# Keys and values of the second memory attention made in the mix and held in DRAM

## The chip, the core and the metric

The kernel runs on one core of one Trainium2 chip. The time is device microseconds of one execution. Three runs of the kernel before took 2700.62, 2703.43 and 2705.85 us, a median of 2703.43 us. A further execution was profiled; all rows below are from it.

## What is computed

Two transformer blocks stand one behind the other, over 512 positions of 1024 features, all in float32. The first has two layers of attention. The second is the one the change is about:

```python
mem_n = rms_norm_2(mem, norm_mem)
h = rms_norm_2(x, norm_mix[l])
p_rw, p_s5, p_gla, p_gate = _split_2(h @ w_in[l], IN_SIZES)
y_rw, y_s5, y_gla = rwkv7_mix(p_rw, ...), s5_mix(p_s5, ...), gla_mix(p_gla, ...)
gates = jax.nn.sigmoid(p_gate).reshape(B, L, N_BRANCH, D_MODEL)
merged = sum(gates[:, :, i] * (y_i @ w_branch[l, i]))
x = x + merged @ w_out[l]
x = x + cross_attention(rms_norm_2(x, norm_xattn[l]), mem_n, xa_wq[l], xa_wkv[l], xa_wo[l])
x = x + conv_ffn(rms_norm_2(x, norm_ffn[l]), ...)
```

In `cross_attention` the queries come from `x`, so from everything before. The keys and values are `mem_n @ wkv`: 256 memory positions, 4 heads of 256 features. They need the kernel's inputs alone.

## The kernel before

Features lie on the 128 partitions, positions along the free axis, in tiles of 128 x 512. A product is made of three TensorE passes (`mm3`, lines 282 to 284): every operand is split into a high part, which ScalarE rounds, and a low part, which VectorE subtracts, and the passes are high by high, high by low, low by high. Weights are split too. `load_split` (lines 307 to 315) loads 256 KB into one of 7 raw buffers (`wraw`) through the queue of SyncE, ScalarE makes `wh` (line 312), VectorE makes `wl` (line 314), each in one of 5 buffers. One such load feeds 12 passes of 512 columns in most of the kernel. For keys and values it feeds 12 passes of 256 columns, because there are 256 memory positions.

The second block's stages are `mix`, `cross` and `ffn`. In `mix` the first branch (RWKV) is the main line of the code: `rwkv_a` for two pairs of heads, then the inverse of small triangles (`rwkv_invert`, 30 dependent steps on VectorE, lines 1506 and 1507), then `rwkv_b` four times. These steps wait on each other, so the code puts other products between them. They come from jobs: generators that yield the TensorE time of the products they have just issued. `push` puts a job in a list, with a kind (0, 1 or 2) and a stream, which names the pool of tiles that it allocates from. `fill(us)` takes products out of the jobs until about that much time has been issued; when no job is ready it gives up, and the main line's next step follows at once. A job that yields a negative number is not ready until the plan's clock has gone on so far. Kind 2 comes first, and kinds 0 and 1 take turns. So the order in which TensorE meets its work is set when the program is built. The framework that builds it then moves independent instructions of one engine past each other, and each engine runs its own list in order.

Jobs of kind 0 in the mix are: the low-rank inputs of RWKV, the gates and merge of branch 1, of branch 2, and the gates of branch 0. Jobs of kind 1 are the S5 branch and behind it the GLA branch. After the last `rwkv_b`, `flush` issues what is left of the jobs, then come the merge of branch 0 (`merge_g`, lines 2206 to 2226) and the product with `w_out`, which adds to `x` (line 1342). Between the four chunks of `w_out` the job `memory` loads and normalises the memory.

In `cross`, head 0's keys, values and queries are made first, in this order. For heads 1 to 3 the queries, keys and values are jobs, and `fill(4.5)` puts their products between the attention's steps; half of the output projection is a job as well. Tiles are allocated from pools by letter, and the last line of the setup of the mix is

```python
kit.room("abcc", a=22, b=11, c=54-22-11)
```

which gives the main line 22 tiles (`a`), jobs of kind 0 11 tiles (`b`), and kinds 1 and 2 together 21 (`c`). `cross` keeps these pools and sends all jobs to `c` (`SFLOW = "accc"`).

Of the kernel before, what the change touches and what calls it, by code (L numbers as in the profile page):

```python
# [10 lines left out]
F32 = mybir.dt.float32  # L11
F32R = mybir.dt.float32r
AF = mybir.ActivationFunctionType
ALU = mybir.AluOpType
# [3 lines left out]
S = 512  # L18
D = 1024
DT = D // 128  # L20
MEM = 256
# [14 lines left out]
BOTH = {"mm": "mm ch si", "si": "si", "ch": "ch"}  # L36
X_BOTH = {"mm": "mm ch", "si": "si", "ch": "mm ch"}
LATE = {"mm": "mm", "si": "si", "ch": "ch", "tr": "ch"}, dict(mm=3, ch=3, si=2)
SFLOW = "accc"
AB_FILL, CD_FILL, X_FILL = (0.9, 1.2), (1.15, 1.3, 1.1), (1.1, 1.4)  # L40


# [607 lines left out]
def tok(b):  # L650
    return lambda a: a[:, b * 128 : b * 128 + 128]
# [3 lines left out]
DENSE_K = [(j * 128, 128, [0, 1, 2, 3]) for j in range(4)]  # L655
# [664 lines left out]
class Second:  # L1320
# [908 lines left out]
    def mix(self):  # L2229
        kit, I = self.kit, self.I  # L2230
        self.xs = kit.xs
        self.merged, self.gates, self.O = {}, {}, []
        gla, s5 = [], []

        def branch1():
            yield from self.s5_g(s5, lambda: kit.push(branch2(), kind=1))
            kit.push(self.merge_g(1, s5, g1))
            self.g2 = kit.push(self.gates_g(2))

        def branch2():  # L2240
            yield from self.gla_g(gla)
            kit.push(self.merge_g(2, gla, self.g2))
            self.g0 = kit.push(self.gates_g(0))

        kit.push(branch1(), kind=1)
        lora = kit.push(self.rwkv_lora())
        g1 = kit.push(self.gates_g(1))
        kit.fill(20.0)
        kit.need(lora)
        rw = self.rwkv()  # L2250
        kit.flush()
        kit.run(self.merge_g(0, rw, self.g0))
        job = kit.push(self.memory(), kind=2, stream=1)
        for c in range(4):
            kit.fill(3, 10)
            kit.run(kit.proj_g(I["w_out"][c], self.O, lambda i, p: self.add(2 * c + i, p, "norm_xattn")))
        kit.need(job)


    def memory(self):  # L2260

        kit, nc, I = self.kit, self.nc, self.I
        ms = self.ms = []
        mems = [kit.load("", src=src) for src in I["mem2T"]]
        yield -6
        for m in range(DT):
            if m % 2 == 0:
                mem, hl = mems[m // 2], kit.u()
            c = slice(m % 2 * MEM, m % 2 * MEM + MEM)
            ms.append([z[:, c] for z in hl])  # L2270
            kit.split_scaled(mem[:, c], self.vec("norm_mem", m), *ms[m])
            if m == 0:
                acc = kit.f(MEM)
                nc.scalar.square(acc, mem[:, c])
            else:
                sq = kit.f(MEM)
                nc.scalar.square(sq, mem[:, c])
                nc.gpsimd.tensor_tensor(acc, acc, sq, op=ALU.add)
            yield -1
        self.mr = kit.t([128, 2], "mr2", 1)  # L2280
        nc.vector.tensor_copy(self.mr, kit.rpow(kit.sums(acc, kit.ones, [tok(0), tok(1)]), 1.0 / D, EPS))
        big = kit.spread_begin(self.mr, 2)
        yield -4
        self.mrb = kit.spread_end(big)

    def cross(self):
        kit, nc, I = self.kit, self.nc, self.I
        xs, ms, mr, mrb = kit.xs, self.ms, self.mr, self.mrb
        st, O = {}, {}
        sc = kit.small(4, "scq")  # L2290

        def keys(h):
            def emit(j, p):
                if not j:
                    hl = kit.u()
                    st["k", h] = [[z[:, j * MEM : j * MEM + MEM] for z in hl] for j in range(2)]
                f = kit.f(MEM)
                nc.vector.tensor_tensor(f, p, mrb, op=ALU.mult)
                kit.split(f, *st["k", h][j])

            yield from kit.proj_g(I["xa_wk"][h], ms, emit)

        def vals(h):
            st["v", h] = []

            def emit(b, p):
                st["v", h].append(kit.u(256))
                kit.split_scaled(p, mr[:, b : b + 1], *st["v", h][b])

            yield from kit.proj_tok_g(I["xa_wv"][h], ms, [tok(0), tok(1)], emit)  # L2310

        def query(h):
            st["q", h] = []

            def emit(j, p):
                st["q", h].append(kit.u())
                if not h and not j:
                    nc.vector.tensor_scalar(sc, kit.rstd(), 256.0**-0.5, None, op0=ALU.mult)
                kit.split(p, *st["q", h][j])

            yield from kit.proj_g(I["xa_wq"][h], xs, emit)

        def out(ts, g=None):
            for t in ts:
                if isinstance(O[t], list):
                    kit.need(O[t])
            for c in range(4):
                w = I["xa_wo"][c][:, :, ts[0] : ts[-1] + 1]
                yield from kit.proj_g(w, [O[t] for t in ts], lambda i, p: self.add(2 * c + i, p, g))

        def done(h, sums):
            s = []

            def end():
                big = kit.inverse(sums)
                yield -2
                rb = kit.spread_end(big)
                for j in range(2):
                    nc.vector.tensor_tensor(s[j], s[j], rb, op=ALU.mult)
                    hl = kit.u()  # L2340
                    kit.split(s[j], *hl)
                    O[2 * h + j] = hl

            def f(outs):
                for j in range(2):
                    s.append(kit.f())
                    nc.scalar.copy(s[j], outs[j])
                O[2 * h] = O[2 * h + 1] = kit.push(end(), True)
                if h == 1:
                    kit.push(out(range(0, 4)))  # L2350

            return f

        kit.run(keys(0))
        kit.run(vals(0))
        kit.run(query(0))
        jobs = [[]] + [[kit.push(g(h)) for g in (query, keys, vals)] for h in range(1, 4)]

        def heads():
            for h in range(4):  # L2360
                kit.need(*jobs[h])
                qk = []
                for (qh, ql), (kh, kl) in zip(st["q", h], st["k", h]):
                    qk += [(qh, kh), (qh, kl), (ql, kh)]
                sums = kit.small(4, "sums")
                soft = kit.soft_full(sc, [sums[:, b : b + 1] for b in range(4)])
                yield Head(kit, qk, st["v", h], [(0, 256)] * 4, DENSE_K[:2], soft, done(h, sums), 4.5)

        kit.attention(heads())
        kit.flush()  # L2370
        kit.run(out(range(4, 8), "norm_ffn"))
# [94 lines left out]
def program(tc, ctx, I, out):  # L2466
    kit = Kit(tc, ctx, I)
# [25 lines left out]
    f.ffn(1, take)  # L2493
    kit.need(job)
    done()
    kit.room("abcc", a=22, b=11, c=54-22-11)
    s.reset = kit.load("reset")
    s.mix()
    kit.flow(SFLOW)
    s.cross()  # L2500
    kit.room("aaaa", a=50)
    s.ffn()
# [14 lines left out]
```

## Time and profile before

| | |
|---|---|
| median of three runs | 2703.43 us (2700.62 to 2705.85) |
| the profiled execution | 2697.67 us |
| its span, first to last instruction | 2695.9 us |
| mean granted TensorE clock | 0.978 of full |
| TensorE busy / weight loads / VectorE / ScalarE / GpSimd | 95% / 77% / 59% / 44% / 19% |

The stages of the second block in the span: the mix's projections and `rwkv_a` until 1650 us, the inverse until 1721, `rwkv_b` until 2068, the merge and `w_out` until 2135, `cross` until 2284, and `ffn` behind it. A matmul's end in the profile is modelled and lies past the start of the next one, so two matmuls that follow each other without a pause look like 100% busy; the distance between their starts is what one costs.

### The profile page before, as it was taken

Reading aid. Unit: us, or ns where it says so; the run is one execution under the profiler, and the core shown is the slowest. Engines: PE = TensorE matmul, PEld = TensorE weight load, DVE = VectorE, ACT = ScalarE, POOL = GpSimd, SP = SyncE. Lnnn points to the kernel's source line nnn. Section 1 sums busy time; section 2 is a strip of 40 time slices with the busy share of each in tenths; the row PEclk is TensorE's granted clock in tenths of the full one; section 3 lists DMA queues with packets and bytes.
Section 4 is the critical chain, followed back from the end, with each engine's and each line's share of the span. In section 5 each row is a group of like instructions: output and inputs, shape, how many; then the busy total and the mean of one; then the engine's idle time right before and its main releaser. Section 6 shows DMA issues by size and latency. Waiting matters only on the chain. (4 is left out here: it accounts for less than half of the span.)

```text
span 2695.9 us, 37069 instructions
## 1 busy us (share of the span) xinstructions
PE 2573.7 (95%) x13432; PEld 2083.8 (77%) x13432; DVE 1594.7 (59%) x3076; ACT 1180.1 (44%) x2208; POOL 518.9 (19%) x439
## 2 busy tenths in 40 slices
PE   8999999999999999999999989799999999999998
PEld 6668778888776787787877767587777798888886
DVE  5686654344457876876335477654464656774673
ACT  5576543233445765332334322435233445543443
POOL 5325021010211131143103232112231300100001
PEclk9999999999999999999999989899999999999999
DMA  4112223333322131334433553421222333233332
GB/s 155 36 51 87 67 85 93 101 97 93 116 89 71 44 98 47 114 118 145 126 106 110 167 170 98 102 97 60 71 79 70 119 119 97 83 97 95 98 94 70
DMA packets 172520, 258.51 MB, mean 96 GB/s; under 512 B 42528, under 2 KB 60832, under 8 KB 172320
## 3 DMA queue, kind: packets, MB, share of 16 engines
q1 hardware_dynamic: 172336, 256.13, 31.2%
q8 instruction: 106, 1.74, 0.3%
q14 instruction: 78, 0.64, 0.1%
HBM read 234.04 MB, written 22.15 MB: 95 GB/s over the span
## 5 line engine op out<-in xcount | busy, mean ns | idle before, releaser
L312 ACT CAST wh<-wraw 128x512 fp32r<-128x512 f32 (+1 forms) x777 | 473.3, 613 | 886.4 <-PE ps_mm L283 606.9
L314 DVE TENSOR_TENSOR wl<-wraw,wh 128x512 fp32r<-128x512 f32 (+1 forms) x691 | 491.7, 715 | 355.5 <-ACT wh L312 343.5
L284 PE MATMUL ps_mm<-xs,wl 128*128 128x512 f32 x1544 | 612.6, 397 | 22.4 <-DVE wl L314 21.5
L282 PE MATMUL ps_mm<-xs,wh 128*128 128x512 f32 x1544 | 623.2, 404 | 9.0 <-ACT wh L312 8.3
L283 PE MATMUL ps_mm<-xs,wh 128*128 128x512 f32 x1544 | 612.6, 397 | 3.0 <-DVE xs L264 2.9
L284 PEld LDWEIGHTS ps_mm<-xs,wl 128*128 128x128 f32 x1544 | 293.8, 190 | 89.6 <-DVE wl L314 24.1
L282 PEld LDWEIGHTS ps_mm<-xs,wh 128*128 128x128 f32 x1544 | 294.1, 190 | 76.4 <-ACT wh L312 8.7
L283 PEld LDWEIGHTS ps_mm<-xs,wh 128*128 128x128 f32 x1544 | 293.6, 190 | 66.2 <-DVE xs L264 6.4
L448 POOL TENSOR_TENSOR acc<-acc,za 128x512 f32<-128x512 f32 x59 | 82.0, 1391 | 729.5 <-ACT za L444 728.2
L282 PE MATMUL ps_mm<-za,wh 128*128 128x512 f32 x460 | 183.2, 398 | 5.6 <-ACT za L248 5.6
L284 PE MATMUL ps_mm<-za,wl 128*128 128x512 f32 x460 | 182.3, 396 | 4.1 <-DVE wl L314 4.1
L283 PE MATMUL ps_mm<-za,wh 128*128 128x512 f32 x460 | 180.7, 393 | 0.2 <-DVE za L245 0.2
L314 POOL TENSOR_TENSOR wl<-wraw,wh 128x512 fp32r<-128x512 f32 x86 | 112.5, 1316 | 304.9 <-ACT wh L312 300.1
L1193 POOL TENSOR_TENSOR za<-za,za 128x512 f32<-128x512 f32 x44 | 60.0, 1364 | 462.0 <-ACT za L1192 462.0
L284 PEld LDWEIGHTS ps_mm<-za,wl 128*128 128x128 f32 x460 | 87.5, 190 | 24.5 <-DVE wl L314 4.5
L282 PEld LDWEIGHTS ps_mm<-za,wh 128*128 128x128 f32 x460 | 87.6, 190 | 24.3 <-ACT za L248 6.4
L282 PE MATMUL ps_mm<-zb,wh 128*128 128x512 f32 (+1 forms) x284 | 100.4, 354 | 4.4 <-ACT zb L248 4.4
L283 PEld LDWEIGHTS ps_mm<-za,wh 128*128 128x128 f32 x460 | 87.3, 190 | 20.5 <-DVE za L245 1.0
L245 DVE TENSOR_TENSOR za<-ps_tr,za 128x512 fp32r<-128x512 f32 (+3 forms) x152 | 84.6, 558 | 31.2 <-ACT za L248 29.9
L283 PE MATMUL ps_mm<-zb,wh 128*128 128x512 f32 (+1 forms) x284 | 97.4, 344 | 0.1
L284 PE MATMUL ps_mm<-zb,wl 128*128 128x512 f32 (+1 forms) x284 | 97.3, 343 | 0.0
L468 POOL TENSOR_TENSOR rs<-sm,neghalf 128x4 f32<-128x4 f32 (+2 forms) x32 | 45.3, 1416 | 240.3 <-DVE sm L467 240.3
(590 smaller groups left out, 4768.2 us busy)
## 6 DMA issues: line engine op xcount, KB each, us to landing
wraw<-w_gu SPq DMA_DIRECT2D x176, 256.0 KB, 2.7
wraw<-w_dn SPq DMA_DIRECT2D x96, 256.0 KB, 2.6
wraw<-w_up SPq DMA_DIRECT2D x88, 256.0 KB, 2.6
wraw<-w_gate SPq DMA_DIRECT2D x48, 256.0 KB, 2.8
wraw<-w_dn SPq DMA_DIRECT2D x48, 192.0 KB, 2.3
dram<-za SPq DMA_DIRECT2D x26, 256.0 KB, 2.5
zc<-dram SPq DMA_DIRECT2D x26, 256.0 KB, 4.5
wraw<-w_cd SPq DMA_DIRECT2D x24, 256.0 KB, 2.7
```

The lines of the kernel that those rows point to most:

```text
L245: self.nc.vector.tensor_tensor(lo, src, hi.bitcast(F32), op=ALU.subtract)
L282: mm(out, ah, bh, start=start, stop=False, **kw)
L283: mm(out, ah, bl, start=False, stop=False, **kw)
L284: mm(out, al, bh, start=False, stop=stop, **kw)
L312: self.nc.scalar.copy(hl[0], raw)
L314: eng.tensor_tensor(hl[1], raw, hl[0].bitcast(F32), op=ALU.subtract)
L448: self.nc.gpsimd.tensor_tensor(self.acc[0], self.acc[0], sq, op=ALU.add)
L468: self.nc.gpsimd.tensor_tensor(r, ms, self.neghalf[:, :n], op=ALU.pow)
L1193: nc.gpsimd.tensor_tensor(a, a, st["rb"], op=ALU.mult)
```

## The change

Keys and values of all four heads become one job of the mix, `memory_kv`, of kind 0, put in the list behind the low-rank job and ahead of the gates of branch 1. It first needs the job `memory`, which is now pushed at the start of the mix. Each finished tile pair (high and low) is stored to a DRAM scratch of 4 heads x 4 tiles of 256 KB, and the store is issued when the first half of the next tile is done (`late`, `store`). Behind the merge of branch 0 the 16 tiles are loaded back into the 18 tiles of pool `b`, for which `SFLOW` makes it stream 2. `cross` then makes queries alone. Its fill is 2.7 in place of 4.5.

```diff
-SFLOW = "accc"
+SFLOW = "acbc"
+C_FILL = 2.7
...
         lora = kit.push(self.rwkv_lora())
+        kit.push(self.memory_kv(kit.push(self.memory(), kind=2, stream=1)))
         g1 = kit.push(self.gates_g(1))
...
         kit.run(self.merge_g(0, rw, self.g0))
-        job = kit.push(self.memory(), kind=2, stream=1)
+        kit.flow(SFLOW)
+        self.kv = []
+        for h in range(4):
+            self.kv.append([kit.r(stream=2) for _ in range(4)])
+            for z, d in zip(self.kv[h], self.kv_dram[h]):
+                kit.nc.sync.dma_start(z.bitcast(F32), d)
         for c in range(4):
-            kit.fill(3, 10)
             kit.run(kit.proj_g(I["w_out"][c], self.O, lambda i, p: self.add(2 * c + i, p, "norm_xattn")))
-        kit.need(job)
...
     def memory(self):
-        mems = [kit.load("", src=src) for src in I["mem2T"]]
-        yield -6
         for m in range(DT):
             if m % 2 == 0:
-                mem, hl = mems[m // 2], kit.u()
+                mem, hl = kit.load("", src=I["mem2T"][m // 2]), kit.u()
+                yield -4
...
+    def memory_kv(self, job):
+        kit, nc, I = self.kit, self.nc, self.I
+        self.kv_dram = self.scratch([4, 4, 128, S])
+        kit.need(job)
+        late = []
+        def store():
+            for z, d in late:
+                nc.sync.dma_start(d, z.bitcast(F32))
+            late.clear()
+        def keys(h):
+            hl = []
+            def emit(j, p):
+                if not j:
+                    hl[:] = kit.u()
+                c = slice(j * MEM, j * MEM + MEM)
+                f = kit.f(MEM)
+                nc.vector.tensor_tensor(f, p, self.mrb, op=ALU.mult)
+                kit.split(f, *(z[:, c] for z in hl))
+                if j:
+                    late.extend((z, self.kv_dram[h, i]) for i, z in enumerate(hl))
+                else:
+                    store()
+            return kit.proj_g(I["xa_wk"][h], self.ms, emit)
+        def vals(h):
...
+        for h in range(4):
+            yield from keys(h)
+            yield from vals(h)
+        yield -3
+        store()
...
     def cross(self):
-        kit.run(keys(0))
-        kit.run(vals(0))
         kit.run(query(0))
-        jobs = [[]] + [[kit.push(g(h)) for g in (query, keys, vals)] for h in range(1, 4)]
+        jobs = [[]] + [[kit.push(query(h))] for h in range(1, 4)]
...
-                yield Head(kit, qk, st["v", h], [(0, 256)] * 4, DENSE_K[:2], soft, done(h, sums), 4.5)
+                yield Head(kit, qk, st["v", h], [(0, 256)] * 4, DENSE_K[:2], soft, done(h, sums), C_FILL)
...
-    kit.room("abcc", a=22, b=11, c=54-22-11)
+    kit.room("abcc", a=22, b=18, c=21)
     s.reset = kit.load("reset")
     s.mix()
-    kit.flow(SFLOW)
     s.cross()
```

Three places show how the order moves. Names are the program's (`wh`, `wl` weights, `xs` the normed input, `zb` and `zc` tiles of the pools, `ps_` PSUM banks); lines of the changed kernel below line 38 are one higher.

TensorE at the end of S5's second half, beside the inverse. Before, the next work is the first projection of GLA (`ps_mm_16169`):

```order
L2159 MATMUL ps_si_15939<-zc_15906,zc_16058 128x63
L2159 MATMUL ps_si_15940<-zc_15906,zc_16058 128x63
L282 MATMUL ps_mm_16169<-xs_13673,wh_16159 128x512
L283 MATMUL ps_mm_16169<-xs_13674,wh_16159 128x512
L284 MATMUL ps_mm_16169<-xs_13673,wl_16160 128x512
```

Now a tile of keys of the last head stands there (`zb_14203` and `zb_14204` are the memory's high and low part):

```order
L2160 MATMUL ps_si_16055<-zc_16035,zc_16258 128x63
L283 MATMUL ps_mm_16278<-zb_14203,wh_16268 128x256
L284 MATMUL ps_mm_16278<-zb_14204,wh_16268 128x256
L2160 MATMUL ps_si_16054<-zc_16032,zc_16303 128x63
L2160 MATMUL ps_si_16055<-zc_16032,zc_16303 128x63
L285 MATMUL ps_mm_16278<-zb_14203,wl_16269 128x256
L283 MATMUL ps_mm_16278<-zb_14203,wh_16268 128x256
```

Between the last `rwkv_a` and the first `rwkv_b`, 192 of the 384 products of keys and values now stand on TensorE; the gates of branch 1, which stood there, come later.

VectorE at the end of the inverse, before. The split of the weights that GLA's projection reads (`wl_16160`) stands behind the last step:

```order
L1506 TENSOR_TENSOR zc_15794<-zc_15793 128x58
L1511 MEMSET zc_15793 128x16
L1507 TENSOR_TENSOR zc_15793<-zc_15793,zc_15794 128x2x29
L1506 TENSOR_TENSOR zc_15794<-zc_15793 128x30
L1507 TENSOR_TENSOR zc_15793<-zc_15793,zc_15794 128x30
L314 TENSOR_TENSOR wl_16160<-wraw_16157,wh_16159 128x512
```

Now splits of weights and of keys stand between the steps (a stretch of the middle):

```order
L1507 TENSOR_TENSOR zc_16133<-zc_16132,zc_16131 128x192
L315 TENSOR_TENSOR wl_16269<-wraw_16266,wh_16268 128x512
L315 TENSOR_TENSOR wl_16275<-wraw_16272,wh_16274 128x512
L1508 TENSOR_TENSOR zc_16132<-zc_16132,zc_16133 128x16x12
L1507 TENSOR_TENSOR zc_16133<-zc_16131 128x26
L315 TENSOR_TENSOR wl_16336<-wraw_16333,wh_16335 128x128
L1508 TENSOR_TENSOR zc_16131<-zc_16131,zc_16133 128x2x13
```

In the 100 rows of VectorE from the first step to the last there was no split of weights before; now there are nine in 110.

TensorE behind the last `rwkv_b`, before. The chain center, sums, spread, gate (`nw`) and merge (`ps_mm_19549`) has nothing between its links:

```order
L1689 MATMUL ps_ch_19504<-za_19502,center_10653 128x512
L460 MATMUL ps_ch_19508<-half_138,za_19506 128x2 x4
L510 MATMUL ps_ch_19520<-ident_136,za_19517 128x128 x4
L282 MATMUL ps_ch_19529<-zb_14378,nw_19531 128x512
L283 MATMUL ps_ch_19529<-zb_14379,nw_19531 128x512
L284 MATMUL ps_ch_19529<-zb_14378,nw_19531 128x512
L282 MATMUL ps_mm_19549<-zc_19539,wh_19545 128x512
```

Now gates of branch 0 (`ps_mm_20060`, `ps_mm_20122`) stand between all of them, here between spread and gate:

```order
L285 MATMUL ps_mm_20060<-xs_14112,wl_20057 128x512
L511 MATMUL ps_ch_20101<-ident_136,za_20086 128x128 x4
L283 MATMUL ps_mm_20122<-xs_13673,wh_20112 128x512
L284 MATMUL ps_mm_20122<-xs_13674,wh_20112 128x512
L285 MATMUL ps_mm_20122<-xs_13673,wl_20113 128x512
L283 MATMUL ps_mm_20122<-xs_13734,wh_20112 128x512
L284 MATMUL ps_mm_20122<-xs_13735,wh_20112 128x512
L285 MATMUL ps_mm_20122<-xs_13734,wl_20113 128x512
L283 MATMUL ps_ch_20132<-zb_14409,nw_20134 128x512
```

Some 120 products of gates that stood before this chain now stand inside it or just behind it.

## Rows read from the trace of the kernel before

**Rows 1.** The page: busy time of each engine (share of the span).

```profile
PE 2573.7 (95%) x13432; PEld 2083.8 (77%) x13432; DVE 1594.7 (59%) x3076; ACT 1180.1 (44%) x2208; POOL 518.9 (19%) x439
```

**Rows 2.** Stretches: length; PE, PEld, DVE, ACT, POOL busy (instructions); clock, DMA share, GB/s.

```profile
1450.00:1650.00 200.00, 182.61 (x879) 146.04 (x877) 127.99 (x218) 67.63 (x108) 61.53 (x46) 0.92 0.46 147
1650.00:1721.00 71.00, 54.82 (x394) 41.22 (x393) 48.95 (x124) 16.04 (x26) 11.89 (x8) 0.90 0.47 112
1721.00:2068.00 347.00, 330.89 (x2452) 273.00 (x2451) 182.58 (x337) 136.85 (x239) 71.20 (x63) 0.99 0.25 78
2068.00:2135.00 67.00, 54.58 (x218) 42.49 (x217) 39.56 (x55) 27.73 (x52) 24.80 (x20) 0.87 0.35 106
2135.00:2284.00 149.00, 148.84 (x910) 132.06 (x909) 83.31 (x164) 72.56 (x144) 6.37 (x5) 1.00 0.36 108
2440.00:2480.00 40.00, 40.00 (x177) 32.80 (x176) 16.76 (x26) 10.86 (x18) 0.00 (x0) 1.00 0.34 97
```

**Rows 3.** TensorE in order of time: start, duration, line, tiles, shape, [idle before].

```profile
1709.78 0.39 PE L282 MATMUL ps_mm<-xs,wh 128*128 128x512 f32 x1
1710.00 0.40 PE L283 MATMUL ps_mm<-xs,wh 128*128 128x512 f32 x1
...
1717.06 0.28 PE L283 MATMUL ps_mm<-wl,xs 128*128 128x256 f32 x1
1717.18 0.28 PE L284 MATMUL ps_mm<-wh,xs 128*128 128x256 f32 x1
```

**Rows 4.** TensorE in order of time, at the end of the inverse.

```profile
1703.03 0.79 PE L284 MATMUL ps_mm<-xs,wl 128*128 128x512 f32 x1 [14.58 <-DVE wl L314]
1703.62 0.63 PE L282 MATMUL ps_mm<-xs,wh 128*128 128x512 f32 x1
1704.05 0.63 PE L283 MATMUL ps_mm<-xs,wh 128*128 128x512 f32 x1
```

**Rows 5.** Waits of TensorE, 1650 to 2135 us: for whom; total us, times, longest.

```profile
PE ps_mm L284 <- DVE wl L314: 14.6, 1, 14.6
PE ps_ch L510 <- DVE za L498: 7.3, 3, 2.6
PE ps_mm L282 <- ACT za L248: 5.6, 2, 3.0
```

**Rows 6.** VectorE, 1661 to 1703 us: all its work, then L1506, then L1507.

```profile
1661.00:1703.00 42.00, 36.62 (x105) 0.88 0.43 104
...
1661.00:1703.00 42.00, 15.03 (x44) 0.88 0.43 104
...
1661.00:1703.00 42.00, 13.23 (x44) 0.88 0.43 104
```

**Rows 7.** VectorE by line and shape: first row 1450 to 1650 us, others 2135 to 2284.

```profile
L314 DVE TENSOR_TENSOR wl<-wraw,wh 128x512 fp32r<-128x512 f32 x48 | 36.9, 780 | 12.1 <-ACT wh L312 12.0
...
L314 DVE TENSOR_TENSOR wl<-wraw,wh 128x512 fp32r<-128x512 f32 x61 | 42.2, 693 | 33.3 <-ACT wh L312 33.1
...
L2298 DVE TENSOR_TENSOR zc<-ps_mm,zb 128x256 f32<-128x256 f32 x6 | 2.5, 424 | 0.3
L245 DVE TENSOR_TENSOR zc<-zc,zc 128x256 fp32r<-128x256 f32 x6 | 2.5, 418 | 0.0
```

**Rows 8.** Waits of SyncE's queue, 1450 to 1721 us.

```profile
SPq L310 <- DVE wl L314: 54.5, 25, 9.4
SPq L2073 <- DVE x L2083: 20.1, 3, 16.3
SPq L2099 <- ACT zc L2164: 17.0, 2, 12.0
```

**Rows 9.** The end of the first block's second memory attention, columns as in rows 2.

```profile
1060.00:1090.00 30.00, 23.85 (x106) 18.59 (x105) 20.23 (x28) 14.54 (x27) 10.44 (x7) 0.94 0.23 71
```

**Rows 10.** DMA issues of the page: count, size, us to landing.

```profile
dram<-za SPq DMA_DIRECT2D x26, 256.0 KB, 2.5
zc<-dram SPq DMA_DIRECT2D x26, 256.0 KB, 4.5
```

More of the change, by code (lines that the diff above doesn't have):

```diff
@@ L2284, in memory, with emit @@
         self.mrb = kit.spread_end(big)
+    def memory_kv(self, job):
[22 more added lines that the diff above has]
+        def vals(h):
+            hl = []
+            def emit(b, p):
+                if not b:
+                    hl[:] = kit.u()
+                c = slice(b * 256, b * 256 + 256)
+                kit.split_scaled(p, self.mr[:, b : b + 1], *(z[:, c] for z in hl))
+                if b:
+                    late.extend((z, self.kv_dram[h, 2 + i]) for i, z in enumerate(hl))
+                else:
+                    store()
+            return kit.proj_tok_g(I["xa_wv"][h], self.ms, [tok(0), tok(1)], emit)
+        for h in range(4):
+            yield from keys(h)
+            yield from vals(h)
+        yield -3
+        store()
@@ L2286, in cross @@
     def cross(self):
         kit, nc, I = self.kit, self.nc, self.I
-        xs, ms, mr, mrb = kit.xs, self.ms, self.mr, self.mrb
+        xs = kit.xs
         st, O = {}, {}
         sc = kit.small(4, "scq")
[L2292 to L2310, printed above, removed]
+        for h, (kh, kl, vh, vl) in enumerate(self.kv):
+            st["k", h], st["v", h] = ([[z[:, j * MEM : j * MEM + MEM] for z in hl] for j in range(2)] for hl in ((kh, kl), (vh, vl)))
         def query(h):
```

## The prediction

> **What bounds the kernel now.** I read the page's busy times first. TensorE is busy for 95% of the span, twice as much as ScalarE [rows 1]. So the change can gain only where TensorE idles, or where its clock is low, and the second view is the table of stretches. It shows where that is. In `cross` TensorE is busy for 148.84 of 149 us at a clock of 1.00; in the inverse 16.2 of 71 us are idle and the granted clock is 0.90 of full; at the merge and `w_out` 12.4 of 67 us are idle at 0.87; in `rwkv_b` 16.1 of 347 at 0.99 [rows 2]. The third view is TensorE in order of time, for the price of a product: starts lie 0.22 us apart at 512 columns and 0.12 at 256 [rows 3]. At the end of the inverse TensorE stands for 14.58 us, and the products behind that wait start 0.43 us apart, which is the 1.2 GHz level of the clock and not 2.4 [rows 4]. So an idle stretch is paid twice, as the wait and as slow products behind it.
>
> The wait was for the low part of a weight. The order of VectorE in the part on the change says why: that split is queued behind the last of the inverse's steps. From 1661 to 1703 us VectorE is busy for 36.62 of 42 us, and the inverse's two lines are 28.3 of it [rows 6]. The second great loss is the chain behind the last `rwkv_b`: waits for `za` and for ScalarE's parts, 7.3 and 5.6 us in all, of up to 3.0 us [rows 5].
>
> So the work that is moved, 384 passes of 256 columns, leaves a stage in which TensorE never stops and goes to stages in which it does. At 0.1175 us each (between the 0.12 of the row and half of 0.22) it is 45 us. No product is added or removed: the total of TensorE's work is the same, and the gain can only be idle time and slow clock. That is the sum's frame, and I work it by stage. Work by stage is products counted in the two orders times the distances above.
>
> **Until the end of `rwkv_a`.** TensorE gets 1 us more work. The memory's loads, squares and splits now stand here and not between the chunks of `w_out`. VectorE has 128 of 200 us busy [rows 2], and the memory adds about 9. Nothing is full, but the memory is one more job that must be ready early. Zero if it is hidden; 8 if all of VectorE's addition becomes a wait; I take +2, nearer to the first, since VectorE is idle for 72 us of the stretch.
>
> **The inverse, 71 us.** 192 of the 384 kv passes come in (22.5 us), gates go out (9.6 us): +12.9 us of work on 49, so 62. That is the floor, and it needs every wait to vanish: 71 to 62 is -9. If nothing that TensorE loses there now is saved, the stage is 71 + 13 = 84. Which is nearer? VectorE decides. A tile of 24 kv passes, 2.8 us of TensorE, wants two splits at 0.78 us and half of a head's keys or values: a multiplication and a subtraction at 0.42 [rows 7], 2.4 us in all. So kv work leans on VectorE at 85% of TensorE's time, where a 512-column job wants one split for 12 x 0.22 = 2.6 us. It is a poor filler beside a VectorE chain. In the stage VectorE goes from 48.95 to about 60 us. But the products now stand in reach: nine splits stand between the steps, so the 14.58 us wait goes, and with it the slow spell behind it (13.65 us at 1.2 GHz, worth half of that). What is late next is the inverse itself: 28.3 us of steps plus some 12 of other VectorE work in what were 42 us. Between 62 and 84 I take 74: floor, plus 12 us of short waits, half of what is lost now. That is +3, bounds -9 and +13.
>
> Here two instructions on the same memory matter. The split took 780 ns in the stretch where GpSimd is busy for 61.53 of 200 us, and 693 ns in `cross`, where GpSimd has 6.37 of 149 [rows 2, 7]. The Trainium skill, SBUF — State Buffer, section "Who interferes with whom", states that a VectorE instruction with two SBUF inputs contends with a GpSimd instruction that reads SBUF; the rows agree in direction, by 87 ns. By that rule the 32 splits that leave `cross` get dearer by 32 x 0.087 = 2.8 us of VectorE, which speaks against the change, though all on an engine that isn't full over the stage.
>
> **The four `rwkv_b`, 347 us.** Work changes by +4.1 us: the other half of kv comes in, gates go out behind the end. 16.1 us are idle now [rows 2], and with slow spells and short gaps some 40 us are lost against products at full distance. The plan of the program had no job ready at places worth 40 us of its clock, and has 26.5 now, a third less. A third of 40 would be 13; part of those places cost nothing, so I take half, 7. -7 + 4 = -3. Bounds: -15 (work hidden entirely in idle time, and more) and +8 (the work, and as much again from kv's VectorE load).
>
> **Merge and `w_out`, 67 us.** Some 27 us of gates now stand in or just behind the chain. They fill its waits: 12.4 us are idle and the clock is 0.87 [rows 2, 5], together some 18 us. I take 11 as saved, since the first links are filled by the order shown and those of `w_out` are now bare: `memory`, which stood there, is gone. +27 - 11 = +16; bounds +9 (all 18 saved) and +27 (none).
>
> **`cross`, 149 us.** 45 us of kv go. TensorE never waits here now, and jobs are fewer: only queries and the output projection fill the softmax's waits. The nearest row for new stalls is the end of the first block's second memory attention, 23.85 of 30 us busy at 0.94 [rows 9]: 6 us idle. I take half and some, 4, between 0 and 12 (twice that row): -45 + 4 = -41, from -45 to -33.
>
> **DMA and SyncE's queue.** 16 stores and 16 loads of 256 KB are added. One takes 2.5 and 4.5 us to land [rows 10], they are off every chain if issued in time, and the DMA share is 0.25 to 0.47 in these stages [rows 2]: zero. The cost would come from the queue's order. SyncE waits for tiles before it issues: 25 times for a raw buffer's release, up to 16.3 us for `x` and 12.0 for S5's tile [rows 8], and a store waits for its tile's split, with the weight loads behind it. A store is issued only at the middle of the next tile, so its tile is then long done: zero, if the raw buffers ahead cover the other waits. The 7 raw and 5 split buffers hold 12 loads, 12 x 12 x 0.1175 = 17 us of kv work, 33 us of 512-column work. The 16 loads back stand behind the last three of the first `w_out` chunks and land under `w_out`'s 67 us.
>
> **The sum.** +2 + 3 - 3 + 16 - 41 = -23 us, so 2697.67 - 23 = 2674.7 us as a profiled execution. The median before lies 5.8 us above the profiled one, so the forecast against it is 2680.5, say 2681. Its own range, from errors of either sign in five terms, is 2666 to 2695.
>
> **Rivals.**
>
> *VectorE becomes the bound and the gain is given back.* For it: 85% of TensorE's time per kv tile, in the stage where VectorE already has 36.62 of 42 us [rows 6]. Against: before and behind those 42 us it has room. Upper bounds of the first two terms, +8 and +13, +4 for `rwkv_b`, +16 and -41: 0, so about 2703.
>
> *SyncE's queue makes it slower.* The stores join a queue that stands for up to 16.3 us [rows 8], against 17 us of cover with kv work. It decides from where one stand is longer than the cover: then TensorE and ScalarE wait for raw weights, not for VectorE. With eight groups of stores, one for each pair of tiles, and about 5 us at each (half of the 9.4 us that the queue waited for a raw buffer), that is +40: -23 + 40 = +17, about 2720. Against: the DMA share leaves room, and TensorE's waits in these stages are for VectorE and ScalarE alone [rows 5].
>
> *Everything goes.* The inverse runs at its floor of 62 (-9), `rwkv_b` at -10, the merge at +12, `cross` at -42, with +2 before: -47, so 2656. For it: what TensorE loses in the mix is some 80 us over these stages, and each wait removed takes a slow spell with it. The Trainium skill, Perfetto Trace Analysis, section "Identifying the Most-Contended Engine", calls the busy share of matmuls a poor measure and prefers that of weight loads. In dense work weight loads are busy for 32.80 of 40 us, 0.82, and in the inverse for 41.22 of 71, 0.58 [rows 2]. By that rule the inverse loses 71 x (1 - 0.58/0.82) = 21 us, not 16, near the 22 that the count of products gives.
>
> That the change does not do what it says I leave out: the order rows show kv between the inverse's steps, and gates in the chain behind `rwkv_b`.
>
> **How the numbers follow.** Forecast 0.62, gain given back 0.14, slower 0.09, everything 0.15. 0.2%, 5.4 us, is about what a measurement of this kernel can tell from no change. Faster by more than that holds for the forecast, for the larger gain and for a sixth of the rival with no gain (0.79); the rest of that rival is within it (0.12); slower is the queue (0.09). The range to hold 8 in 10 goes from 2662 (some of the larger gain) to 2702 (half of the case without gain).
>
> **What would show it.** In the profile of the changed kernel: no wait of over 5 us for `wl` in the inverse, and a clock near 1.00 in its last 15 us; the stage 70 to 78 us long, with VectorE over 80% busy. The chain behind the last `rwkv_b` without waits over 2 us, but waits and slow clock at the first chunks of `w_out`. `cross` 108 us long, with idle time of some us where there was none. TensorE waiting for raw weights (`wraw`, by a DMA) anywhere in the mix would be the queue. Wrong is the forecast if `cross` loses over 10 us, or if the inverse is over 80 us long.

## The result and the profile after

The changed kernel takes 2723.32 us (median of 4 runs, 2721.62 to 2731.04), against 2703.89 us for the kernel before: ratio 1.0078, 95% interval 1.0063 to 1.0093. It is 19.4 us slower, where 23 us less was forecast. The profiled execution is the longest of the four, 2731.04 us. Some 14 us of its length lie in the first block, whose instructions stand in the same order in both kernels. So the stretches behind it are compared; they add up to 18.2 us, near the 19.4 of the medians. In that block, in the same order, one execution lost up to 7 us on the other within 400 products, so stage differences of a few us between single executions are not to be leaned on. The lines of the kernel after are numbered one higher than those of before, from the change on (its L313 is L312 of before).

The page of the kernel after, busy time of each engine, answers to [rows 1]:

```profile
PE 2606.6 (96%) x13432; PEld 2104.3 (77%) x13432; DVE 1588.7 (58%) x3076; ACT 1176.9 (43%) x2206; POOL 520.7 (19%) x439
```

The number of products is the same, yet TensorE is busy for 33 us more, some of it in the first block. "Busy" got longer without more work, so look at the clock next. Stretches of the kernel after, with the columns of [rows 2]: from the second `rwkv_a`'s triangular products to the first `rwkv_b` (it holds the inverse), the first part of that, the four `rwkv_b`, merge and `w_out`, and `cross`:

```profile
1651.60:1771.50 119.90, 98.25 (x629) 81.28 (x629) 81.04 (x186) 36.19 (x63) 15.06 (x10) 0.81 0.55 157
1651.60:1680.00 28.40, 26.67 (x196) 21.59 (x197) 17.06 (x37) 3.97 (x8) 1.96 (x2) 0.64 0.31 98
1771.50:2128.00 356.50, 338.18 (x2468) 272.47 (x2467) 177.88 (x334) 134.89 (x236) 71.80 (x63) 0.98 0.24 74
2127.90:2230.05 102.15, 97.67 (x418) 78.39 (x417) 48.25 (x74) 38.25 (x63) 24.12 (x16) 0.97 0.46 147
2230.05:2350.70 120.65, 119.85 (x593) 98.81 (x592) 69.31 (x130) 59.75 (x117) 8.26 (x7) 1.00 0.23 70
```

The same bounds in the kernel before (the first, fourth and fifth of these; `rwkv_b` is in [rows 2]):

```profile
1638.80:1721.10 82.30, 66.12 (x460) 49.57 (x459) 59.88 (x151) 19.17 (x31) 11.89 (x8) 0.92 0.46 115
2067.70:2152.70 85.00, 72.58 (x296) 57.16 (x295) 48.06 (x67) 35.21 (x64) 28.69 (x23) 0.90 0.34 103
2152.70:2317.30 164.60, 164.42 (x983) 144.33 (x982) 100.11 (x189) 85.69 (x166) 9.62 (x8) 1.00 0.34 103
```

The last two rows are what was wanted: `cross` is 43.9 us shorter, merge and `w_out` 17.1 longer, with a clock of 0.97 where it was 0.90. The loss is in the first row: 82.3 us became 119.9, at a clock of 0.81 instead of 0.92. I call it "the inverse's stretch". Counted as in the prediction (products by their distances at full clock, an estimate), its work went from 59.6 to 73.9 us and what is lost on top from 22.7 to 46.0. Of that loss 16.2 us were idle before and 21.6 are now: most of the added loss is slow clock. In the second row TensorE runs at 0.64, so mostly at 1.2 GHz, though it is busy for 26.67 of 28.4 us; ahead of this spell it waited twice for a triangle that VectorE had to mask, 2.12 and 1.73 us.

Waits of TensorE in the inverse's stretch after (for whom; total us, times, longest), to hold against [rows 5], three largest:

```profile
PE ps_mm L283 <- ACT wh L313: 13.4, 4, 7.6
PE ps_ch L1485 <- DVE za L1440: 3.9, 2, 2.1
PE ps_mm L285 <- DVE wl L315: 3.4, 2, 1.9
```

The wait for `wl` of 14.58 us [rows 4] is gone, as forecast. In its place stand waits for `wh`, the high part of a weight, made by ScalarE as soon as the raw weight is there. Two of them, in order of time on TensorE:

```profile
1695.83 0.79 PE L283 MATMUL ps_mm<-wh,zb 128*128 128x256 f32 x2 [3.23 <-ACT wh L313]
...
1697.51 0.41 PE L284 MATMUL ps_mm<-wl,zb 128*128 128x256 f32 x1
1697.72 0.41 PE L285 MATMUL ps_mm<-wh,zb 128*128 128x256 f32 x1
...
1733.53 0.80 PE L283 MATMUL ps_mm<-wh,zb 128*128 128x256 f32 x2 [7.58 <-ACT wh L313]
```

Behind the first wait the products of 256 columns start 0.21 us apart; at full clock it was 0.12 [rows 3]. Why was `wh` late? ScalarE says it for two of the casts:

```profile
1688.02 0.62 ACT L313 CAST wh<-wraw 128x512 fp32r<-128x512 f32 x1 [2.94 <-DMA wraw<-xa_wk]
...
1732.23 0.63 ACT L1766 ACTIVATE zc<-zc 128x512 f32<-128x512 f32 x1 [0.87 <-DVE zc L1761]
...
1732.87 2.16 ACT L313 CAST wh<-wraw 128x512 fp32r<-128x512 f32 x4
```

The first cast waited for the raw weight itself, and so did the one behind the 3.23 us. The later ones, behind the 7.58 us, stood in ScalarE's own queue behind an activation that waited for VectorE; their raw weights had been issued at 1719.54 us. So TensorE's waits for raw weights are 4.8 of the 13.4 us, and whether the 7.58 us go back to SyncE's queue too is not followed here. The raw weights come by SyncE. Its queue in order of time:

```profile
1670.03 1.77 SPq L2100 DMA_DIRECT2D dram<-zc  x4
1679.32 0.34 SPq L1466 DMA_DIRECT2D dram<-za  x1
1679.70 2.83 SPq L2100 DMA_DIRECT2D dram<-zc  x6
...
1683.54 2.00 SPq L311 DMA_DIRECT2D wraw<-xa_wk  x1
...
1687.97 3.69 SPq L1499 DMA_DIRECT2D zc<-dram  x7
1691.70 1.91 SPq L311 DMA_DIRECT2D wraw<-xa_wv  x4
```

Nothing is issued between 1671.80 and 1679.32 us. The stores that end the gap are not kv's own: L1466 writes out triangles of `rwkv_a` (I call it the spill), L2100 writes S5's outputs. The key weight of 1683.54 us stands behind both, and the value weights of 1691.70 behind those and the loads of the inverse (L1499). What its stores in question waited for from 1574 to 1772 us, after, beside [rows 8] (the largest sum there is still that of loads for a raw buffer, 34.4 us in 21 waits):

```profile
SPq L1466 <- DVE za L1436: 14.5, 2, 13.9
SPq L1466 <- DVE za L1460: 13.8, 2, 7.4
SPq L2100 <- ACT zc L2165: 9.7, 2, 5.9
```

The same stores waited as long before, 38 us in all: 20.7 for the spill (L1465, 1559 to 1721 us) and 17.0 for S5's outputs [rows 8]. What is new is what stands behind them.

### The profile page after: what moved, and what is told of

Read it like the earlier page. It is cut to its first block, busy times and chain, and to the rows that moved or that the text cites. A ratio compares the mean times of both kernels' runs of the same rounds, so it can differ in the third digit from the quotient of the medians.

```text
span 2729.2 us, 37118 instructions
## 1 busy us (share of the span) xinstructions
PE 2606.6 (96%) x13432; PEld 2104.3 (77%) x13432; DVE 1588.7 (58%) x3076; ACT 1176.9 (43%) x2206; POOL 520.7 (19%) x439
## 5 line engine op out<-in xcount | busy, mean ns | idle before, releaser
L313 ACT CAST wh<-wraw 128x512 fp32r<-128x512 f32 (+1 forms) x777 | 472.4, 613 | 898.5 <-PE ps_mm L284 607.0
L283 PEld LDWEIGHTS ps_mm<-xs,wh 128*128 128x128 f32 x1544 | 295.0, 191 | 85.1 <-ACT wh L313 17.1
L283 PE MATMUL ps_mm<-zb,wh 128*128 128x512 f32 (+1 forms) x284 | 103.1, 363 | 6.0 <-ACT zb L249 4.4
```

Source lines behind the costliest of these rows:

```text
L283: mm(out, ah, bh, start=start, stop=False, **kw)
L313: self.nc.scalar.copy(hl[0], raw)
```

## The experiments

Times are medians, ratios are to the kernel before, with their 95% interval. "Stretch" is the inverse's stretch, 82.3 us before and 119.9 after; "tail" is what follows the last `rwkv_b`, up to the last product, 619.2 and 592.7.

**Another place for the whole work.** The memory and kv go behind the merge of the first branch, and the gates of the third branch start with kv's first tile:

```
-            self.g2 = kit.push(self.gates_g(2))
+            kit.push(self.memory_kv(self.memory()))
...
-        kit.push(self.memory_kv(kit.push(self.memory(), kind=2, stream=1)))
...
-        kit.need(job)
+        yield from job
+        self.g2 = kit.push(self.gates_g(2))
```

> Memory, keys and values put in the list behind the merge of branch 1, so that all 384 products stand in rwkv_b; rwkv_a and the inverse keep the order of the kernel before. Theory 1 (the loss is the meeting with the inverse: its loads, its stores and S5's share SyncE's queue with the weights of keys and values): the stretch from the second rwkv_a's lower products to the first rwkv_b is 82 us long again, where it took 120 in the changed kernel, cross keeps its gain, and the time is 2672 to 2690 us. Rival (products of 256 columns are a poor filler in the mix wherever they stand, since VectorE and the weights cannot follow): rwkv_b grows by 55 us or more instead, 2700 us or more.

2690.05 us, 0.9947 (0.9931 to 0.9964): faster than both kernels, at the upper end of the range expected. Its stretches, from the first `rwkv_a`'s triangular products on (columns as in [rows 2]): until the first `rwkv_b`, the four `rwkv_b`, merge and `w_out`, `cross`:

```profile
1559.30:1721.10 161.80, 132.90 (x804) 102.85 (x803) 116.14 (x239) 44.67 (x70) 40.10 (x29) 0.88 0.46 136
1721.10:2099.80 378.70, 361.60 (x2789) 308.25 (x2789) 213.46 (x398) 156.79 (x292) 79.05 (x71) 0.99 0.33 104
2099.80:2186.60 86.80, 82.16 (x348) 65.26 (x347) 42.14 (x65) 32.53 (x54) 24.47 (x16) 0.96 0.47 155
2186.60:2307.30 120.70, 119.90 (x593) 98.80 (x592) 69.31 (x130) 59.71 (x117) 8.21 (x7) 1.00 0.22 70
```

The first row is as long as before (161.9). `rwkv_b` takes in 34.5 us of work and grows by 32.1: nearly nothing is hidden there, though the plan has a job ready at every place now. The gain comes where gates fill the merge's waits: 82.16 of 86.8 us busy, against 72.58 of 85.0, for 1.8 us more. So the harm of the change lies in the early place. The memory moved late together with kv, so this run doesn't part the two.

**Stores off SyncE's queue, all of them.** The spill, S5's outputs and the inverse's results are issued by GpSimd, in the kernel after:

```
-                nc.sync.dma_start(d, z)
+                nc.gpsimd.dma_start(d, z)
...
-                nc.sync.dma_start(places(self.inv[1], q)..., m[g][s])
+                nc.gpsimd.dma_start(places(self.inv[1], q)..., m[g][s])
...
-                nc.sync.dma_start(dst[...], v8(y)[16 * q : 16 * q + 16])
+                nc.gpsimd.dma_start(dst[...], v8(y)[16 * q : 16 * q + 16])
```

> The changed kernel with four groups of stores issued by GpSimd and not by SyncE: the spill of rwkv_a's tiles, S5's outputs and the inverse's two results. What TensorE computes and its list of jobs stay. Theory 1 (queue of SyncE): the inverse's first step comes about 20 us earlier after rwkv_a, its results reach DRAM within 8 us of its last step (now 32), the stretch shrinks from 120 to under 100 us, and the time is 2695 to 2708 us. Rival (VectorE and narrow products bound the stretch): it stays within 8 us of 120, 2717 to 2728 us.

2705.67 us, 1.0004 (0.9995 to 1.0013), 17.7 under the kernel after. The stretch falls to 105.7, not under 100, and TensorE waits for no `wh` in it. The same edit in the kernel before:

> The same move of four groups of stores on the kernel before, a control. Theory 1: there SyncE's queue held the inverse back little, 4 us at its end, so 2696 to 2706 us. If this gains as much as the move does in the changed kernel, the queue isn't what the change made worse.

2712.16 us, 1.0031 (1.0019 to 1.0043), above the range expected: there it costs 8 us. So the 17.7 are not a good that the move does to any kernel; without kv behind them the stores stood well where they were.

**The memory early, kv late.** In the kernel before, the memory is loaded and split at the mix's start, kv stays in `cross`, and the pools are cut as after:

```
+        kit.need(kit.push(self.memory(), kind=2, stream=1))
...
-    kit.room("abcc", a=22, b=11, c=54-22-11)
+    kit.room("abcc", a=22, b=18, c=21)
```

> The kernel before with the memory's loads, norm and splits made at the start of the mix and pool b of 18 tiles; keys and values stay in cross. Theory 1: this part costs little, 2700 to 2712 us. Rival: it is the memory's work on VectorE and ScalarE that delays rwkv_a, 2712 to 2722 us.

2720.64 us, 1.0056 (1.0036 to 1.0076): slower by 16.5 us, inside the rival's range, but not where the rival put it. Between the two `rwkv_a` nothing is lost (76.7 us against 79.6); the stretch has 9 us more and `rwkv_b` 10, with no product of keys or values there:

```profile
1645.00:1736.50 91.50, 72.49 (x450) 53.33 (x450) 61.93 (x151) 17.92 (x29) 13.87 (x10) 0.83 0.40 103
1736.50:2092.90 356.40, 336.26 (x2454) 277.99 (x2454) 180.66 (x337) 136.45 (x239) 71.12 (x63) 0.97 0.24 75
```

The wait for `wl` is as before (14.7 us). To part the pools from the memory, the kernel before gets the pools of after, with 9 of the 18 tiles held idle through the mix:

```
+        hold = [kit.f(stream=1) for _ in range(9)]
+        for z in hold:
+            kit.nc.gpsimd.memset(z[:, :8], 0.0)
```

> The kernel before with pool b of 18 tiles of which 9 are held, without use, from the start of the mix to its last job, as the early memory held them; the memory itself stays late. It leaves 9 free where there were 11. If the early memory's 16 us came from the pool, 2714 to 2724 us; if from its own work in rwkv_a (VectorE later by 2 us, and waits and slow clock behind that), 2700 to 2708 us.

2709.67 us, 1.0024 (1.0011 to 1.0036), between the two ranges. The pools cost some 5 us, in `rwkv_b` (+3.2) and the tail (+3.7), none in the stretch. The other 12 us of the memory early stay unexplained: in the stretch TensorE is idle for 19.0 us instead of 16.2, and the rest of what it loses (33.3 against 22.7) is slow clock.

**Is the inverse itself late?** Its loads stand behind kv's and are issued 36 us after the start of the stretch, where it was 9 before (at 1687.5 and 1647.7 us). Here they are moved ahead by 14 rows of SyncE's queue:

```
+        with kit.tc.high_priority():
             for q in range(4):
                 for g in range(2):
                     nc.sync.dma_start(m[g][32 * q : 32 * q + 32], ...)
```

> The changed kernel with one thing moved: on SyncE's queue the eight loads of the inverse's triangles stand 14 rows earlier, ahead of the spill that waited for VectorE until 1679 us and of 14 stores of S5. Theory 1 (queue): the loads are issued about 15 us earlier (1672 and not 1687 us) and the inverse starts and ends as much earlier; alone, 2708 to 2718 us, since its results still stand behind weight loads. Rival (VectorE is full and TensorE's products are narrow): within 4 us of the changed kernel's 2723.

2741.13 us, 1.0131 (1.0101 to 1.016), above both ranges. The inverse ends 71 us after the start of the stretch and not 83 (at 1715.4 and 1734.5 us), and the kernel is 18 us slower than after. So an earlier inverse alone gains nothing; what a late one costs the run can't tell, since another wait came in. TensorE's waits in the stretch, the two largest:

```profile
PE ps_mm L285 <- DVE wl L315: 18.5, 1, 18.5
PE ps_mm L283 <- ACT wh L313: 10.9, 4, 7.5
```

VectorE, in order of time:

```profile
1699.14 0.39 DVE L1509 TENSOR_TENSOR zc<-zc,zc 128x224 f32<-128x224 f32 x1
1699.45 0.68 DVE L315 TENSOR_TENSOR wl<-wraw,wh 128x512 fp32r<-128x512 f32 x1
```

The old wait is back: the split that TensorE needs at 1681 us comes at 1699.45, behind the inverse's steps (L1508, L1509). The inverse's results moved ahead as well, with `high_priority(300)` around their stores:

> As the run before, and the eight stores of the inverse's first result stand together behind the first weights of GLA and no longer between weights of gates, 14 to 20 rows earlier on SyncE's queue. Theory 1: the results are stored within 10 us of the last step, the stretch from the second rwkv_a to the first rwkv_b falls from 120 to 95 to 105 us, 2700 to 2712 us in all. Rival: 2719 or more, and the stretch stays over 112 us.

2740.63 us, 1.013 (1.0103 to 1.0156): no difference to the one before, and on the rival's side (the stretch is 121.2 us long).

**Is VectorE the bound?** During the inverse the low parts of weights are made by GpSimd, in the kernel after and in the one with kv behind the merge:

```
+        kit.by(kit.nc.gpsimd)
         while inverse[0]:
             kit.fill(2.0)
+        kit.by(kit.nc.vector)
```

> The changed kernel with the low parts of those weights that are loaded while the inverse is planned made by GpSimd and not by VectorE. Rival theory (VectorE is the bound beside the inverse): VectorE loses some 10 splits of 0.69 us there, and the time falls by 8 us or more, to 2715 or less. Theory 1 (queue of SyncE): 2718 to 2730 us, since the inverse's loads and stores stand where they stood, and a split takes 1.3 us on GpSimd.

2735.64 us, 1.0114 (1.0086 to 1.0142): 12 us slower than after, above both ranges.

> The kernel with keys and values behind the merge of branch 1 (2690 us), and the low parts of the weights that are loaded while the inverse is planned made by GpSimd, not VectorE. There TensorE stands for 14.6 us for such a split, which VectorE has behind the inverse, and the clock is at its lower level for 14 us after it. If that queueing is the whole cause, most of 20 us go: 2668 to 2678 us. Rival (GpSimd's splits and the inverse on VectorE hinder each other, or another wait takes the place): 2684 to 2694 us.

2702.94 us, 0.9989 (0.9974 to 1.0004): 13 us slower than without the edit, above both ranges too. TensorE's longest wait there:

```profile
PE ps_si L283 <- ACT zc L249: 15.8, 1, 15.8
```

The wait for `wl` (14.6) was swapped for one of 15.8 us for ScalarE, behind another step of VectorE. Giving the splits to GpSimd shortens nothing, in either kernel. That doesn't clear VectorE: a split takes GpSimd some 1.3 us, VectorE some 0.7.

**What is an idle stretch worth?** In the kernel with kv behind the merge, 65 products of 512 columns that nobody reads are issued wherever the plan had no job during the inverse:

```
+            for _ in range(5):
+                kit.nc.tensor.matmul(bank[0], w, x, start=True, stop=True)
```

> The kernel with keys and values behind the merge of branch 1 (2690 us), where TensorE stands for 14.6 us at the end of the inverse; where the program's plan has no job ready there, 65 passes of 512 columns are added that nobody reads, 14.8 us at full clock, so that TensorE works instead of standing. If the slow spell behind the wait (13.65 us at the 1.2 GHz level) is the price of the standing, it goes and the time falls by half of it: 2681 to 2686 us, though work was added. If the clock does not hang on it, 2689 to 2694 us.

2690.59 us, 0.995 (0.9933 to 0.9968), the same as without them. The stretches of the old wait with them:

```profile
1690.00:1700.00 10.00, 10.00 (x87) 6.99 (x86) 9.17 (x25) 0.00 (x0) 0.00 (x0) 1.00 0.00 0
1700.00:1710.00 10.00, 9.26 (x36) 6.74 (x35) 7.28 (x20) 7.77 (x12) 0.00 (x0) 0.85 0.34 51
```

and in the kernel before:

```profile
1690.00:1700.00 10.00, 0.00 (x0) 0.00 (x0) 9.14 (x26) 0.00 (x0) 0.00 (x0) 0.63 0.52 100
1700.00:1710.00 10.00, 6.97 (x20) 4.49 (x21) 7.31 (x19) 3.95 (x7) 0.00 (x0) 0.69 0.51 132
```

TensorE is busy and at 1.00 where it stood, 13.1 us of idle time are gone (16.2 to 3.1), and the stretch is no shorter: 85.5 us against 82.3. In the kernel before, the granted clock was low mainly while nothing ran, where it costs nothing.

**The decisive pair.** Only the two stores that stand in front of kv's weights go to GpSimd, the spill and S5's outputs; the inverse's results stay on SyncE. In the kernel after:

```
-                nc.sync.dma_start(d, z)
+                nc.gpsimd.dma_start(d, z)
...
-                nc.sync.dma_start(dst[...], v8(y)[16 * q : 16 * q + 16])
+                nc.gpsimd.dma_start(dst[...], v8(y)[16 * q : 16 * q + 16])
```

> The changed kernel with the spill of rwkv_a and S5's outputs stored by GpSimd; the inverse's loads and stores stay with SyncE. If the gain of the run that moved four groups (18 us) came from weights of keys and values that no longer stand behind those stores, TensorE's 13 us of waits for them go here too, without GpSimd's 2.5 us for each store of the inverse: 2696 to 2706 us. If it came from the inverse's results, 2716 us or more.

2698.7 us (10 runs), 0.9977 (0.9967 to 0.9986): 24.6 us under the kernel after, and 5 to 6 under before, where 23 were forecast. The stretch takes 103.1 us, and the four `rwkv_b` behind it 358.0:

```profile
1634.50:1737.60 103.10, 93.45 (x665) 79.97 (x664) 82.75 (x181) 35.67 (x64) 35.20 (x48) 0.88 0.63 188
1737.60:2095.60 358.00, 338.00 (x2476) 272.46 (x2476) 182.31 (x347) 136.41 (x238) 71.49 (x63) 0.99 0.25 74
```

The edit moved more than two stores, because the framework ordered each engine's list anew. In this kernel the second `rwkv_a`'s triangular products stand ahead of more of kv's (285 passes of 256 columns in the stretch, 240 in the kernel after), and the inverse ends at 1744.0 us, behind the end of the stretch. A fairer measure begins at the first `rwkv_a`'s triangular products, since then all of kv lies inside. The rows are the kernel before, the kernel after and this one:

```profile
1559.20:1721.10 161.90, 132.94 (x804) 102.80 (x803) 116.22 (x239) 44.82 (x70) 40.17 (x29) 0.88 0.47 136
1574.10:1771.50 197.40, 162.20 (x1050) 137.72 (x1049) 139.11 (x280) 60.37 (x105) 40.38 (x28) 0.84 0.54 166
1567.80:1737.60 169.80, 152.05 (x1040) 130.23 (x1039) 131.87 (x267) 58.76 (x103) 60.74 (x71) 0.88 0.59 182
```

That is 27.6 us less than in the kernel after, with 17.4 us less of idle time.

TensorE's waits in the stretch, all that are 2 us or more in sum:

```profile
PE ps_si L2160 <- DVE zc L2141: 3.6, 2, 3.2
PE ps_ch L1393 <- POOL zc L1778: 3.3, 1, 3.3
PE ps_ch L1485 <- DVE za L1440: 2.3, 1, 2.3
```

No wait for `wh` and none for `wl` is left, and the stores now hold up another queue (GpSimd in order of time):

```profile
1658.91 2.26 POOL L2100 DMA_DIRECT2D dram<-zc  x4 [16.93 <-ACT zc L2165]
...
1664.43 0.60 POOL L1466 DMA_DIRECT2D dram<-za  x1 [3.26 <-DVE za L1460]
```

GpSimd now stands before these stores (16.93 us idle ahead of the first), and less hangs on it: TensorE's one wait for it here is 3.3 us. The control is the same edit in the kernel with kv behind the merge:

> The same move in the kernel with keys and values behind the merge of branch 1, a control: TensorE waits there for VectorE, not for weights that come late, so no gain, 2686 to 2698 us. A gain of over 8 us would mean that SyncE's queue held the old order back as well.

2692.1 us, 0.9957 (0.994 to 0.9974), 2 us above the same kernel without the edit. Where kv's weights don't stand behind these stores, moving them gains nothing. So the 24.6 us belong to the meeting of the two, kv's weight loads behind stores that wait for their tiles. How much of it comes through the new order of the lists was not parted.

## Why the prediction was wrong, point by point

| Term | Forecast, us | Measured, us |
|---|---|---|
| until the end of `rwkv_a` (first part: 79.6 to 77.5) | +2 | -2 |
| the inverse (82.3 to 119.9) | +3 | +38 |
| the four `rwkv_b` (346.6 to 356.1) | -3 | +10 |
| merge and `w_out` (85.0 to 102.1) | +16 | +17 |
| `cross` (164.6 to 120.7) | -41 | -44 |
| sum | -23 | +18 |

My stretches begin at an event that both kernels have (the triangular products of the second `rwkv_a`, the end of the last `rwkv_b`), so the second row begins 11 us earlier than the prediction's 71 us, and the boundary between the last two lies at 2153 and not at 2135 us, which is inside `w_out`.

**The inverse is the first step that failed.** The work that comes in was right: 14.3 us counted, 12.9 forecast. The wait for `wl` went, as forecast. What failed is "half of what is lost now" is saved: the loss doubled instead, from 22.7 to 46.0 us. One part of the error is shown by runs, another is not.

*SyncE's queue, 24.6 us in the whole.* The prediction put the DMA and queue term at zero, "if the raw buffers ahead cover the other waits", with a cover of 17 us of kv work. That was the right condition with a wrong test. Single stands of 13.9 and 7.4 us are shorter than 17; but shorter ones and other issues stand between them, with the inverse's loads behind, so that four weights were loaded between 1640.9 and 1691.7 us, and one in the last 20 us of that. And I looked for who waits now in [rows 5]: in the kernel before nobody waited for `wh`, since 512-column products need a weight each 2.6 us and kv's one each 1.4 (12 products at 0.12). It was the rival "SyncE's queue makes it slower": sign and mechanism (TensorE and ScalarE wait for raw weights) are right, but the stores in front are those of `rwkv_a` and S5, not kv's eight groups, and it had a chance of 0.09. That its 2720 lies beside the measured 2723.32 is luck: it put 40 us on the queue, where clearing the queue gained 24.6, and the rest of the miss lies elsewhere.

*What is left with the queue cleared: 18 us, cause open.* From the first `rwkv_a`'s triangles to the end of the last `rwkv_b` the kernel before takes 508.5 us and the one with two stores moved 527.8: 19.3 more, for some 18 us more work. Nothing is absorbed on balance, where the prediction had +2. By stage, the part up to the first `rwkv_b` takes 7.9 more (forecast +5), `rwkv_b` 11.4 (forecast -3), and the tail 26 less, as forecast (-25). So with the queue cleared the first two terms nearly hold, and `rwkv_b` is the miss.

In the first of these parts 11.2 us of idle time went (29.0 to 17.8), but the loss to slow clock grew by some 7 us (21 to 28, by the count). And "an idle stretch is paid twice" was too dear: of the slow spell of 13.65 us that the prediction put behind the wait for `wl`, most lay inside the wait (0.63 from 1690 to 1700 us, with no product running). The run with products that nobody reads shows it: 14.7 us of work, by the count, made the stretch 3.2 us longer, and the time did not fall.

*The memory made early* was priced at +2, in `rwkv_a`. Its own stage got no longer (-2), but alone, without kv, it cost 16.5 us, in the stretch and in `rwkv_b`; some 5 of these are the pools. That is near the 18 us that are missing. Whether it is the same loss is not shown: no run has kv early and the memory's cost removed. Nor is it shown how much of the rest is VectorE, the rival "VectorE becomes the bound"; giving the splits to GpSimd made both kernels slower and settles nothing.

**`rwkv_b` is the second step that failed.** It was to gain 7 us because the plan has fewer places without a job, 26.5 us of its clock instead of 40. By the count its loss was 40.6 us before and 46 after, and 38.5 in the kernel with kv behind the merge, whose plan has no such place in `rwkv_b`. The plan's dry places are not TensorE's idle time. The 10 us are 4 of work and 5 of loss. The 4 were forecast, but from a wrong reading: no "other half of kv" comes in. In the kernel after, all 384 passes start between 1608.7 and 1742.3 us, ahead of the first `rwkv_b`; what came in are passes of 512 columns (814 against 793). So kv's own products are not in `rwkv_b` to slow it. The memory early, without kv, lost 10 us there at equal work, tiles held idle alone 3.2.

**Merge, `w_out` and `cross`** came out within 3 us, for the reasons given: gates fill the chain's waits (idle 12.4 to 4.5 us, longest wait 2.2), and `cross` has nearly no stalls with fewer jobs (119.85 of 120.65 us busy). The expected waits at the first chunks of `w_out` did not come.

**The second reading of the loss by weight loads.** The Trainium skill, Perfetto Trace Analysis, section "Identifying the Most-Contended Engine", prefers the busy share of weight loads. Before, it gave 21 us for the inverse where the count gave 22. After, by the same reckoning, 119.9 x (1 - 0.68/0.82) = 21 us, and the count gives 46. Here the measurement decides, and the share fails for two reasons. A weight load takes 188 ns for 256 columns as for 512 (`cross`, before), so kv's products raise the share without using TensorE better (0.88 in `cross` with kv, 0.82 without). And at the low clock a load is longer: some 300 to 330 ns for kv's loads from 1660 to 1672 us, after, so the slow clock, most of the added loss, doesn't show in the share.

What stays open: why the memory alone, early, costs 12 us besides the pools; where `rwkv_b`'s 40 us go; and why TensorE ran at 0.64 for 28.4 us at the start of the stretch, after, ahead of the stretch's first wait for a weight (28.4 x 0.36, an estimate of 10 us).

## What to carry to other kernels

A queue that issues DMAs in order is a resource of its own: before you put loads behind stores that wait for their tiles, list what stands ahead of each load there, add up the stands that follow each other, and hold them against the time between two loads of the new work, not of the old. Price what the moved work needs beforehand as a change of its own: the memory made early looked like 2 us and cost 16.5. Products that need no other engine went into an idle stretch nearly free (65 passes for 3.2 us); kv's, with the queue cleared, took 7.9 us there for some 12 of work, and what they gained was lost again in `rwkv_b`. The waits that paid were the merge's (2690.05 us). When an edit moves the order, measure between events that hold the same work in both kernels. Moving one instruction ahead in one in-order queue may only show the next queue's order: here a wait of 18.5 us came in once, and one of 15.8 us took another's place.

## What the runs showed of the hardware

GpSimd issued the inverse's small scattered stores one by one, about 2.5 us apart (the run with all stores moved; GpSimd in order of time):

```profile
1736.68 0.66 POOL L1519 DMA_DIRECT2D dram<-zc  x1 [3.81 <-issue]
1739.21 0.65 POOL L1519 DMA_DIRECT2D dram<-zc  x1 [1.88 <-issue]
```

On SyncE two of them take 0.95 us. The 16 take some 40 us, which may be why moving three stores gained 7 us less than moving two.

The granted clock was 0.64 for 28.4 us in which TensorE was busy for 94% (second stretch of the kernel after), behind two waits of 2.12 and 1.73 us. A wait of 14.58 us, in the kernel before, was followed by 18 us at 0.91. The length of a wait did not tell the cost behind it.
